# First S5 layer: inputs turned up ahead of the outputs, one token tile's GLU products moved, a fourth of Q on GpSimd

## The chip, the cores and the metric

The kernel runs on one core of one Trainium2 chip. The metric is the time of one execution on the device in microseconds (us); less is better. An engine named PE in the profile is TensorE, DVE is VectorE, ACT is ScalarE, POOL is GpSimd, and SP is the queue of SyncE, which issues most DMA transfers.

## What is computed

A trunk of four layers over 512 tokens with 1024 channels in float32: a layer with an S5 mixer, one with gated linear attention, one with differential attention and a second S5 layer, each followed by a SwiGLU FFN of hidden width 2816. The change touches only the first S5 mixer:

```python
def s5_mixer(h, lam_re, lam_im, log_dt, b_re, b_im, c_re, c_im, d_skip, w_glu):
    ...
    def chunk_step(carry, u_c):
        s_re0, s_im0 = carry
        bu_re = jnp.einsum('bcgh,gph->bcgp', u_c, bb_re)
        bu_im = jnp.einsum('bcgh,gph->bcgp', u_c, bb_im)
        ...
        _, _, s_re, s_im = lax.associative_scan(_cdiag_combine, (a_re, a_im, bu_re, bu_im), axis=1)
        s_re = s_re + p_re * s_re0[:, None] - p_im * s_im0[:, None]
        s_im = s_im + p_re * s_im0[:, None] + p_im * s_re0[:, None]
        y = jnp.einsum('bcgp,ghp->bcgh', s_re, cr) - jnp.einsum('bcgp,ghp->bcgh', s_im, ci)
        return (s_re[:, -1], s_im[:, -1]), y
    ...
    y = y + d_skip.astype(f32) * h.astype(f32)
    z = jax.nn.gelu(y).astype(h.dtype)
    a, b = jnp.split(z @ w_glu, 2, axis=-1)
    return a * jax.nn.sigmoid(b)
```

The 1024 channels are 64 groups of 16, each with a diagonal complex state of 64.

## The kernel before

The kernel is one long program, layer after layer. In the first S5 layer (`s5_first`) nothing can be prepared ahead, so the operators of the recurrence are computed beside the layer's own work. Four tokens at a time are handled as one wide step of the recurrence, so that the scan has 128 columns for each of 4 blocks.

The layer runs through eight parts of 128 channels. `s5_pipe` goes through ten steps (`kk`, called step 0 to 9 here) and in each works on several parts at once. The functions inside it, with the name by which the profile's rows can be recognised:

- `up(kk)`: four transposes turn part kk of the normed input into a PSUM bank (tile `up`, line 1392), and ScalarE copies it into `room` (line 1405).
- `products(kk)`: 16 recorded products with the input operators `inm` give V (line 1413), the inputs of the states.
- `states(kk)`, `scan`, `turn`: VectorE's rotation of V by the phases `cs` into `mods` (lines 1418 to 1423), two scans (line 1427) and four products into `prods` (lines 1436 and 1440).
- `outputs(kk)`: TensorE's y (lines 1447 and 1449) from `room` and `prods`, and ScalarE's gelu into z (line 1451; the profile calls the tile `z` or `gain`).
- `turned(kk)`: four transposes of z into a bank (tile `zp`, line 1464) and ScalarE's cast to its high half (line 1465). `rest(kk)`: VectorE's low half (line 1469). Both read the bank.
- `glu(kk)`: the products of the turned outputs with the GLU weights, for four token tiles (`NT` is 4), three products each (`mm3`, lines 420 to 422).

`s5_first` gives it hooks, functions that `s5_pipe` calls at named places of a step. They prepare the operators: `ins` turns X (tile `xps`, line 1214) and copies it into `inm` (line 1237); `phases` makes the angles (`rough`, `angle` on TensorE, lines 1032 to 1042; copies and sines on ScalarE, lines 1034 to 1050, with a table load where sines follow a gelu); `s5_rows` makes rows of the skip operator (tile `rps`, line 1180), which `s5_map` sends through DRAM; `decays` makes `r4`; `new_x` makes X on GpSimd, `new_q` makes Q. `s5_qt` turns the raw C matrices (tile `cps`, line 1118), ScalarE copies them into Q (line 1139, `base`, `Q[h][1]`), and two groups of three operations multiply them by powers (lines 1072 to 1074; `Q[h][2]` and `Q[h][3]`). There are four X and four Q, numbered h, for two parts each. `out_pads` brings Q into the output operators `oms` with four DMAs of SP's queue. `high` and `low` split the staged weights in two halves on ScalarE (line 392) and VectorE (line 400).

What sets the order: `self.hand_all()` puts all engines into an order written out by hand. Each engine does its instructions in the order in which the program emits them, and waits at each for its data and for a free buffer. PSUM has eight banks in three rings:

```python
    def acc(self, name="acc"):
        return self.ps.tile([P, 512], F32, tag="acc", name=name, bufs=4)
    def sbank(self, name="sb"):
        return self.ps.tile([P, 512], F32, tag="s", name=name, bufs=2)
    def tp(self, name="tp"):
        return self.ps.tile([P, 4, P], F32, tag="tp", name=name, bufs=2)
```

`up`, `xps`, `cps`, `rps`, y and `zp` all come from `tp`, so from two banks in turn: whoever takes one waits until the one two places before has been read. V comes from `sbank`; angles and the GLU's sums come from `acc`. The engine that multiplies Q is an argument:

```python
    def s5_q(self, eng, pool, L, b0, nb, bufs=1):
        Q = pool.tile([P, 2, nb, 5, 16], F32, tag="Q", name="Q", bufs=bufs)
        f = lambda *r: self.cross(eng, pool, L, b0, nb, *r, "dq")
```

Behind the ten steps follow the rest of the GLU (`s5_glu`) and the first FFN. The order of emission in step kk is: high(weights) in even steps, the hook "first" (rps, decays), states(kk), low(weights), outputs(kk-1), the hook "operators" (angles, xps of part kk+1), up(kk+2), turned(kk-1), products(kk+1), scans and turns, the hook "beside" (cps, Q), rest(kk-1), staging of weights, glu(kk-2).

Of the kernel before, what the change touches and what calls it, by code (L numbers as in the profile page):

```python
# [24 lines left out]
NT = SEQ // P  # L25
# [42 lines left out]
class Left:  # L68
# [4 lines left out]
    early = False  # L73
# [79 lines left out]
class Sides(Left):  # L153
# [4 lines left out]
    early = True  # L158
# [154 lines left out]
class Trunk:  # L313
# [1053 lines left out]
    def s5_pipe(self, L, hu, zT, natural, room, get, before=None, hooks=None, steps=None, left=None):  # L1367
# [4 lines left out]
        nc = self.nc  # L1372
# [14 lines left out]
        def up_first(kk):  # L1387
            ps = self.acc("up")[:].rearrange("p (b m) -> p b m", b=4) if left and kk in (1, 2, 3) else self.tp("up")[:]
            ups[kk] = ps
            for b in range(4):  # L1390
                g0 = 8 * kk + 2 * b
                nc.tensor.transpose(
                    ps[:, b], hu[:, g0 : g0 + 2].rearrange("p g t c -> p (g t c)"), self.ident[:]
                )

        def up(kk):
            if kk not in ups:
                up_first(kk)
            ps, o = ups[kk], room[kk % 4]
            if left and kk < 4:  # L1400
                v.tensor_tensor(
                    o.rearrange("p (b m) -> p b m", b=4), ps, left.Rt.unsqueeze(1).broadcast_to([P, 4, P]), op=ALU.mult
                )
            else:
                nc.scalar.copy(o, ps.rearrange("p b m -> p (b m)"))

        def products(kk):

            U, inm = room[kk % 4], get(kk, "in")
            V[kk] = [self.sbank("V"), self.sbank("V")]  # L1410
            for z in range(2):
                for b in range(4):
                    mm(V[kk][z][:, bs(b)], inm[:, z, bs(b)], U[:, bs(b)], start=True, stop=True)  # L1413

        def states(kk):

            cs, m = get(kk, "cs"), hold[kk % 2][0]
            v.tensor_tensor(m[:, 0], V[kk][0][:], cs[:, 0], op=ALU.mult)
            v.tensor_tensor(m[:, 3], V[kk][0][:], cs[:, 1], op=ALU.mult)
            v.tensor_tensor(m[:, 1], V[kk][1][:], cs[:, 1], op=ALU.mult)  # L1420
            v.tensor_tensor(m[:, 2], V[kk][1][:], cs[:, 0], op=ALU.mult)
            v.tensor_tensor(m[:, 0], m[:, 0], m[:, 1], op=ALU.add)
            v.tensor_tensor(m[:, 2], m[:, 2], m[:, 3], op=ALU.subtract)

        def scan(kk, z):
            m = hold[kk % 2][0]
            v.tensor_tensor_scan(m[:, 1 + 2 * z], get(kk, "r4"), m[:, 2 * z], 0.0, op0=ALU.mult, op1=ALU.add)
# [14 lines left out]
        def outputs(kk):  # L1442

            U, om, mop, q = room[kk % 4], get(kk, "out"), get(kk, "map"), hold[kk % 2][1]
            yb = self.tp("y")
            for b in range(4):
                mm(yb[:, b], U[:, bs(b)], mop[:, bs(b)], start=True, stop=False)
                for j in range(4):
                    mm(yb[:, b], q[:, j, b], om[:, j // 2, bs(b)], start=False, stop=j == 3)  # L1449
            z = room[4 + kk % 2].rearrange("p (t n) -> p t n", t=4)  # L1450
            nc.scalar.activation(
                z.rearrange("p t (g h) -> p g t h", h=16),
                yb[:].rearrange("p b (g t h) -> p (b g) t h", t=4, h=16), AF.Gelu_apprx_tanh,
            )
# [5 lines left out]
        def turned(kk):  # L1460
            z = room[4 + kk % 2].rearrange("p (t n) -> p t n", t=4)
            zps[kk] = zp = self.tp("zp")
            for t in range(4):
                nc.tensor.transpose(zp[:, t], z[:, t], self.ident[:])
            self.last_turned = nc.scalar.copy(dst(kk)[0], zp[:])

        def rest(kk):
            d = dst(kk)
            v.tensor_tensor(d[1], zps[kk][:], d[0].bitcast(F32), op=ALU.subtract)

        def glu(kk):
            if not accs:
                accs.extend(self.acc() for _ in range(NT))
            hl = hls[kk // 2]
            for t in range(NT):
                ts = slice(t * P, (t + 1) * P)
                self.mm3(
                    accs[t][:], zT[:, 0, kk, ts], zT[:, 1, kk, ts], hl[:, 0, kk % 2], hl[:, 1, kk % 2],
                    kk == 0, kk == KT - 1,
                )  # L1480

        if hooks:
            hook = lambda name, kk: hooks[name](kk) if name in hooks else None
            early = hooks.get("early", ())
            self.hand_all()
            if left:
                for kk in range(4):
                    up_first(kk)
            before(up, products)
            for kk in range(10):  # L1490
                if kk % 2 == 0 and kk:
                    hls[kk // 2 - 1] = self.high(stage[kk // 2 - 1], 2, 512)
                hook("first", kk)
                if kk < 8:
                    states(kk)
                if kk == 7:
                    rest(5)
                hook("ahead of low", kk)
                if kk % 2 == 0 and kk:
                    self.low(hls[kk // 2 - 1], stage[kk // 2 - 1])  # L1500
                hook("behind states", kk)
                if 1 <= kk < 9:
                    outputs(kk - 1)
                hook("operators", kk)
                late = left and kk + 2 < 4
                if kk + 2 < 8 and not late:
                    up(kk + 2)
                hook("ahead of zp", kk)
                if 1 <= kk < 9:
                    turned(kk - 1)  # L1510
                hook("behind zp", kk)
                if kk == 8:
                    glu(6)
                if kk + 1 < 8:
                    products(kk + 1)
                hook("behind products", kk)
                if kk < 8:
                    scan(kk, 0)
                    scan(kk, 1)
                    hook("behind scans", kk)  # L1520
                    for k in range(4):
                        turn(kk, k)
                if late:
                    up(kk + 2)
                hook("ahead of rest", kk)
                if kk in early:
                    rest(kk - 1)
                hook("beside", kk)
                if 1 <= kk < 9 and kk != 6 and kk not in early:
                    rest(kk - 1)  # L1530
                if kk % 2 == 0 and kk < 8:
                    stage[kk // 2] = self.staged(self.wb_src(wg, kk, D), 2, 512)
                if kk >= 2 and kk != 8:
                    glu(kk - 2)
                hook("last", kk)
            self.hand()
            return accs
# [33 lines left out]
    def s5_first(self, ctx):  # L1571
        nc, i = self.nc, self.i
# [4 lines left out]
        with self.tc.tile_pool(name="s5_0", bufs=1) as p:  # L1577
# [16 lines left out]
            X, Q, ph, r4 = {}, {}, {}, {}  # L1594
# [4 lines left out]
                    f()  # L1599

            def new_q(h):
                Q[h] = self.s5_q(nc.vector, p, 0, 8 * h, 8, 2)
                Q[h][1](self.s5_qt(raw[h][1]))

            rounded, *rows = self.s5_rows_of_phases(p)
            for y in inm:
# [33 lines left out]
            def phases(*pieces):  # L1640
                for kk, name in pieces:
                    if name == "rough":
                        ph[kk] = self.s5_phases_first(kk, cs(kk))
                    ph[kk][name]()
# [8 lines left out]
            def out_pads(kk):  # L1653
                self.s5_out_pads(oms[kk % 2], Q[kk // 2][0], slice(4 * (kk % 2), 4 * (kk % 2) + 4))
# [75 lines left out]
            def beside(kk):  # L1730
                h = kk // 2
                if kk == 2:
                    phases((7, "clip"))
                if kk % 2 == 0 and kk < 6:
                    self.s5_b_pads(bp, X[h + 1][0])
                if kk % 2 == 0 and kk < 6:
                    new_q(h + 1)
                if kk == 2:
                    phases((4, "sines"), (5, "sines"))
                if kk % 2 and kk < 7:  # L1740
                    Q[h + 1][2]()
                    Q[h + 1][3]()
                    out_pads(kk + 1)
                if kk == 1:
                    phases((4, "clip"), (5, "clip"))

            rv = {}
            hooks = {
                "first": first, "early": (2, 4), "ahead of low": ahead_of_low, "ahead of rest": ahead_of_rest, "operators": operators, "behind states": behind_states, "ahead of zp": ahead_of_zp, "behind zp": behind_zp,
                "behind products": behind_products, "behind scans": behind_scans, "beside": beside,  # L1750
            }
            accs = self.s5_pipe(0, hu, zT, True, room, get, before, hooks)
# [722 lines left out]
```

## Time and profile before

| | us |
|---|---|
| median of three runs | 2287.49 (2284.28 to 2288.44) |
| profiled execution, its own time | 2292.27 |
| its span | 2290.6 |
| TensorE busy | 2215.2 (97%) |
| VectorE busy | 1582.7 (69%) |
| ScalarE busy | 1111.4 (49%) |
| GpSimd busy | 322.7 (14%) |
| stage from 57 to 114 us: TensorE, VectorE, ScalarE, GpSimd busy | 53.63, 51.25, 37.17, 23.79 of 57 |

How to read it: a row of a timeline has the start from the span's begin, the time from the first to the last end of the merged instructions, engine, line, operation, output tile and input tiles with their shapes, and how many instructions were merged. In brackets stands how long the engine had been idle before, and what ended the wait. TensorE's products are pipelined, so that a row's length has its last product's way through the array in it; the distance from start to start tells what a group costs. In rows of a stretch of time the columns are its length, the busy time of TensorE with its instructions, the granted clock as a share of the full one, the busy share of the DMA engines and what they moved in GB/s. A matmul in float32 counts as two instructions.

### The profile page before, as it was taken

The page shows a single profiled execution, that of the slowest core. Times are in us where ns is not written, and L with a number is a line of the kernel's source. Part 1 is how long each engine was busy: PE and PEld are TensorE (multiplying, and loading weights), DVE is VectorE, ACT ScalarE, POOL GpSimd, SP SyncE. Part 2 cuts the span into 40 slices and gives each one's busy share as a digit, 9 for nine tenths or more (in the row PEclk, how much of TensorE's full clock was granted, in tenths as well). Part 3 has the DMA queues.
Part 4 walks back from the last instruction along what each step waited for, and adds up shares of the span by engine and source line. Part 5 has one row for each costly group of instructions (what it writes and reads, how often), then busy time and mean ns, then how long its engine had stood idle before and what let it go on. Part 6 is the DMA issues. An engine that isn't in the chain of part 4 may idle for free. (4 is left out here: it accounts for less than half of the span.)

```text
span 2290.6 us, 37251 instructions
## 1 busy us (share of the span) xinstructions
PE 2215.2 (97%) x14871; PEld 1966.9 (86%) x14871; DVE 1582.7 (69%) x2412; ACT 1111.4 (49%) x1779; POOL 322.7 (14%) x444
## 2 busy tenths in 40 slices
PE   6999999999999999999999999999999899999998
PEld 5888979889787799998988887899999788989997
DVE  9865878776525488777745675976766864957675
ACT  6634645444443355555435675654534223634443
POOL 5401142421000110100002231110000100101000
PEclk8999999999999999999999999999999999999999
DMA  4256666663322556765246464976641555766622
GB/s 89 59 168 170 161 158 177 162 179 89 115 76 67 147 152 175 184 172 150 94 143 147 101 148 129 234 201 146 166 101 47 143 152 147 194 174 154 169 74 74
DMA packets 294503, 319.91 MB, mean 140 GB/s; under 512 B 70141, under 2 KB 233241, under 8 KB 294202
## 3 DMA queue, kind: packets, MB, share of 16 engines
q1 hardware_dynamic: 231706, 235.79, 33.9%
q0 software_dynamic: 62624, 81.75, 19.2%
q8 instruction: 117, 1.92, 0.3%
q14 instruction: 56, 0.46, 0.1%
HBM read 285.62 MB, written 16.65 MB: 132 GB/s over the span
## 5 line engine op out<-in xcount | busy, mean ns | idle before, releaser
L400 DVE TENSOR_TENSOR whl<-wst,whl 128x1024 fp32r<-128x1024 f32 x272 | 331.9, 1225 | 273.2 <-ACT whl L392 271.1
L392 ACT CAST whl<-wst 128x1024 fp32r<-128x1024 f32 x272 | 284.5, 1051 | 345.3 <-PE acc L422 248.7
L563 PE MATMUL a<-side,whl 128*128 128x256 f32 x3168 | 382.9, 277 | 6.1 <-DVE whl L400 6.0
L563 PEld LDWEIGHTS a<-side,whl 128*128 128x128 f32 x3168 | 370.3, 188 | 7.9 <-DVE whl L400 6.8
L420 PE MATMUL acc<-whl,act 128*128 128x512 f32 x704 | 278.1, 395 | 1.7 <-DVE g L608 1.2
L421 PE MATMUL acc<-whl,act 128*128 128x512 f32 x704 | 274.9, 390 | 0.0
L422 PE MATMUL acc<-whl,act 128*128 128x512 f32 x704 | 274.8, 390 | 0.0
L563 PE MATMUL c<-side,whl 128*128 128x256 f32 x2112 | 256.2, 278 | 7.2 <-DVE whl L400 7.2
L563 PEld LDWEIGHTS c<-side,whl 128*128 128x128 f32 x2112 | 248.4, 189 | 8.2 <-DVE whl L400 8.2
L400 DVE TENSOR_TENSOR whl<-slot,whl 128x1024 fp32r<-128x1024 f32 x105 | 127.9, 1223 | 65.9 <-ACT whl L392 65.4
L420 PEld LDWEIGHTS acc<-whl,act 128*128 128x128 f32 x704 | 132.1, 188 | 31.4 <-DVE g L608 1.7
L422 PEld LDWEIGHTS acc<-whl,act 128*128 128x128 f32 x704 | 132.2, 188 | 27.9
L421 PEld LDWEIGHTS acc<-whl,act 128*128 128x128 f32 x704 | 132.2, 188 | 26.0 <-issue 0.2
L392 ACT CAST whl<-slot 128x1024 fp32r<-128x1024 f32 x105 | 110.1, 1053 | 74.4 <-PE acc L422 28.2
L420 PE MATMUL acc<-whl,hT 128*128 128x512 f32 x352 | 143.0, 406 | 1.0 <-DVE ro L2204 1.0
L422 PE MATMUL acc<-whl,hT 128*128 128x512 f32 x352 | 138.3, 393 | 0.0
L421 PE MATMUL acc<-whl,hT 128*128 128x512 f32 x352 | 138.3, 393 | 0.0
L563 PE MATMUL d<-sides,whl 128*128 128x256 f32 x1056 | 133.4, 283 | 1.3 <-ACT whl L392 1.3
L563 PE MATMUL a<-sides,whl 128*128 128x256 f32 x1056 | 134.0, 283 | 0.6 <-DVE x L546 0.6
L563 PEld LDWEIGHTS a<-sides,whl 128*128 128x128 f32 x1056 | 129.4, 191 | 1.7 <-issue 1.0
L563 PEld LDWEIGHTS d<-sides,whl 128*128 128x128 f32 x1056 | 128.9, 191 | 1.9 <-ACT whl L392 1.9
L599 POOL DMA_DIRECT2D wst<-in_ffn_w_gate_up_dram x44 | 57.1, 1297 | 441.8 <-DMA wst<-in_ffn_w_gate_up_dram 139.0
(458 smaller groups left out, 3933.4 us busy)
## 6 DMA issues: line engine op xcount, KB each, us to landing
wst<-in_ffn_w_gate_up_dram SPq DMA_DIRECT2D x88, 512.0 KB, 4.5
wst<-in_ffn_w_down_dram SPq DMA_DIRECT2D x88, 512.0 KB, 4.7
slot<-in_ffn_w_gate_up_dram SPq DMA_DIRECT2D x69, 512.0 KB, 6.2
wst<-in_ffn_w_gate_up_dram POOLq DMA_DIRECT2D x44, 512.0 KB, 6.0
halves<-in_ffn_w_gate_up_dram SPq DMA_DIRECT2D x42, 512.0 KB, 5.4
wst<-in_s_w_glu_dram SPq DMA_DIRECT2D x32, 512.0 KB, 4.8
wst<-in_gla_w_in_dram SPq DMA_DIRECT2D x24, 512.0 KB, 3.6
wst<-in_diff_w_qkv_dram SPq DMA_DIRECT2D x24, 512.0 KB, 4.3
```

Source lines behind the costliest of these rows:

```text
L392: self.last["high"] = self.nc.scalar.copy(hl[:, 0], w[:])
L400: self.last["low"] = self.nc.vector.tensor_tensor(hl[:, 1], w[:], hl[:, 0].bitcast(F32), op=ALU.subtract)
L420: mm(out, lh, rh, start=first, stop=False)
L421: mm(out, lh, rl, start=False, stop=False)
L422: self.last["mm"] = mm(out, ll, rh, start=False, stop=last)
L563: mm(o, hl[:, x, k, c], side[:, y, k], start=first and not (j or k or n), stop=k == 3 and n == 2, skip_group_check=True,)
L599: nc.gpsimd.dma_start(w[:], left.quarter(*plus, b), accum_op=ALU.add)
```

## The change

Three things are done in the first S5 layer alone; a new hook entry `apart` turns on the first two.

1. In steps 1 to 5 `up(kk+2)` is emitted at the start of the step (behind `high`, ahead of the hook "first"), no longer behind the hook "operators".
2. In steps 2 to 6 the GLU products of the first token tile, three of the twelve, are emitted behind `turned` and ahead of `products(kk+1)`; the other nine stay at the end of the step.
3. Q number 3, the last fourth, is made on GpSimd, and its two groups are emitted at once in step 4 behind its copies; before they were emitted in step 5 on VectorE. Its `out_pads` stay in step 5.

```diff
--- before.py
+++ after.py
@@ -1468,11 +1468,11 @@
             d = dst(kk)
             v.tensor_tensor(d[1], zps[kk][:], d[0].bitcast(F32), op=ALU.subtract)
 
-        def glu(kk):
+        def glu(kk, tiles=range(NT)):
             if not accs:
                 accs.extend(self.acc() for _ in range(NT))
             hl = hls[kk // 2]
-            for t in range(NT):
+            for t in tiles:
                 ts = slice(t * P, (t + 1) * P)
                 self.mm3(
                     accs[t][:], zT[:, 0, kk, ts], zT[:, 1, kk, ts], hl[:, 0, kk % 2], hl[:, 1, kk % 2],
@@ -1482,6 +1482,7 @@
         if hooks:
             hook = lambda name, kk: hooks[name](kk) if name in hooks else None
             early = hooks.get("early", ())
+            apart = hooks.get("apart", False)
             self.hand_all()
             if left:
                 for kk in range(4):
@@ -1490,6 +1491,10 @@
             for kk in range(10):
                 if kk % 2 == 0 and kk:
                     hls[kk // 2 - 1] = self.high(stage[kk // 2 - 1], 2, 512)
+                late = left and kk + 2 < 4
+                soon = apart and kk and kk + 2 < 8
+                if soon:
+                    up(kk + 2)
                 hook("first", kk)
                 if kk < 8:
                     states(kk)
@@ -1502,8 +1507,7 @@
                 if 1 <= kk < 9:
                     outputs(kk - 1)
                 hook("operators", kk)
-                late = left and kk + 2 < 4
-                if kk + 2 < 8 and not late:
+                if kk + 2 < 8 and not late and not soon:
                     up(kk + 2)
                 hook("ahead of zp", kk)
                 if 1 <= kk < 9:
@@ -1511,6 +1515,10 @@
                 hook("behind zp", kk)
                 if kk == 8:
                     glu(6)
+
+                parted = apart and 2 <= kk < 7
+                if parted:
+                    glu(kk - 2, (0,))
                 if kk + 1 < 8:
                     products(kk + 1)
                 hook("behind products", kk)
@@ -1531,7 +1539,7 @@
                 if kk % 2 == 0 and kk < 8:
                     stage[kk // 2] = self.staged(self.wb_src(wg, kk, D), 2, 512)
                 if kk >= 2 and kk != 8:
-                    glu(kk - 2)
+                    glu(kk - 2, range(1 if parted else 0, NT))
                 hook("last", kk)
             self.hand()
             return accs
@@ -1599,8 +1607,11 @@
                     f()
 
             def new_q(h):
-                Q[h] = self.s5_q(nc.vector, p, 0, 8 * h, 8, 2)
+                Q[h] = self.s5_q(nc.gpsimd if h == 3 else nc.vector, p, 0, 8 * h, 8, 2)
                 Q[h][1](self.s5_qt(raw[h][1]))
+                if h == 3:
+                    Q[h][2]()
+                    Q[h][3]()
 
             rounded, *rows = self.s5_rows_of_phases(p)
             for y in inm:
@@ -1738,15 +1749,16 @@
                 if kk == 2:
                     phases((4, "sines"), (5, "sines"))
                 if kk % 2 and kk < 7:
-                    Q[h + 1][2]()
-                    Q[h + 1][3]()
+                    if h < 2:
+                        Q[h + 1][2]()
+                        Q[h + 1][3]()
                     out_pads(kk + 1)
                 if kk == 1:
                     phases((4, "clip"), (5, "clip"))
 
             rv = {}
             hooks = {
-                "first": first, "early": (2, 4), "ahead of low": ahead_of_low, "ahead of rest": ahead_of_rest, "operators": operators, "behind states": behind_states, "ahead of zp": ahead_of_zp, "behind zp": behind_zp,
+                "first": first, "early": (2, 4), "apart": True, "ahead of low": ahead_of_low, "ahead of rest": ahead_of_rest, "operators": operators, "behind states": behind_states, "ahead of zp": ahead_of_zp, "behind zp": behind_zp,
                 "behind products": behind_products, "behind scans": behind_scans, "beside": beside,
             }
             accs = self.s5_pipe(0, hu, zT, True, room, get, before, hooks)
```

## The prediction

> **What bounds the kernel now.** I read the page first, then the waits of TensorE in the stage that is edited (44 to 150 us), then that stage's timelines engine by engine. Times are us from the start of the span, durations the second column; in brackets stands the idle time before.
>
> ```profile
> span 2290.6 us, 37251 instructions
> PE zp L1464 <- ACT inm L1237: 3.2, 5, 0.7
> PE V L1413 <- ACT inm L1237: 0.7, 1, 0.7
> ```
>
> TensorE hardly idles in this stage: once a step the turning of the outputs (zp, line 1464) waits 0.7 us for ScalarE's copies of the input operators (inm), and once, in step 6, V does (columns: total, times, longest). Those six waits, 3.9 us, are all that the change can take out on TensorE. The order around one of them, steps 1 and 2:
>
> ```profile
> 47.62 1.98 PE L1118 MATMUL cps<-ident,craw 128*64 128x128 f32 x16
> 49.52 0.80 PE L1447 MATMUL y<-scr,room 128*128 128x128 f32 x2
> ...
> 55.32 0.49 PE L1040 MATMUL angle<-counts,frow 12*128 12x512 f32 x1
> ...
> 57.68 1.15 PE L1214 MATMUL xps<-ident,X 64*64 64x64 f32 x32
> 58.76 0.66 PE L1392 MATMUL up<-ident,scr 128*128 128x128 f32 x4
> 60.10 0.66 PE L1464 MATMUL zp<-ident,gain 128*128 128x128 f32 x4 [0.68 <-ACT inm L1237]
> 60.59 1.95 PE L1413 MATMUL V<-room,inm 128*128 128x128 f32 x16
> 62.48 0.50 PE L1032 MATMUL rough<-counts,frow 12*128 12x512 f32 x1
> ...
> 63.61 0.69 PE L1180 MATMUL rps<-Q,bpad 128*32 128x64 f32 x32
> 64.23 0.49 PE L1447 MATMUL y<-scr,room 128*128 128x128 f32 x2
> ...
> 68.90 0.50 PE L1040 MATMUL angle<-counts,frow 12*128 12x512 f32 x1
> ...
> 74.16 1.95 PE L1413 MATMUL V<-room,inm 128*128 128x128 f32 x16
> ...
> 77.06 0.50 PE L420 MATMUL acc<-whl,zT 128*128 128x512 f32 x1
> ...
> 79.95 0.39 PE L1447 MATMUL y<-scr,room 128*128 128x128 f32 x2
> ...
> 106.16 0.39 PE L1447 MATMUL y<-scr,room 128*128 128x128 f32 x2
> ...
> 118.27 0.69 PE L1180 MATMUL rps<-Q,bpad 128*32 128x64 f32 x32
> ```
>
> ```profile
> 51.34 1.12 ACT L1139 ACTIVATE Q<-cps 64x128 f32<-64x128 f32 x4
> 58.88 1.17 ACT L1237 COPY inm<-xps 64x512 f32<-64x512 f32 x2 [2.06 <-PE xps L1214]
> 60.07 0.58 ACT L1405 COPY room<-up 128x512 f32<-128x512 f32 x1
> 60.80 1.10 ACT L1465 CAST zT<-zp 128x512 fp32r<-128x512 f32 x1
> 63.25 0.69 ACT L1034 ACTIVATE turns<-rough,magic 128x512 f32<-128x512 f32 x1 [1.35 <-PE rough L1033]
> ...
> 65.93 1.03 ACT L392 CAST whl<-wst 128x1024 fp32r<-128x1024 f32 x1
> 66.86 0.61 ACT L1058 COPY r<-s5r 128x512 f32<-128x512 f32 x1
> ...
> 77.18 1.13 ACT L1139 ACTIVATE Q<-cps 64x128 f32<-64x128 f32 x4 [1.73 <-PE cps L1118]
> ...
> 85.14 0.60 ACT L1451 ACTIVATE gain<-y 128x512 f32<-128x512 f32 x1
> ...
> 106.37 1.11 ACT L1139 ACTIVATE Q<-cps 64x128 f32<-64x128 f32 x4
> ```
>
> The reader is to see how these go through the two banks of the pool `tp`, handed out in turn. In order of emission they are up(2), cps(1), y(0), xps(2), up(3), zp(0), rps(1), y(1): zp(0) has the bank of xps(2), and starts at 60.10, right after the inm copies end (58.88 + 1.17 = 60.05). So the banks are the hidden resource, and each is freed by the engine that reads it, mostly ScalarE in its own order.
>
> VectorE is the second bound:
>
> ```profile
> 75.48 1.10 DVE L1469 TENSOR_TENSOR zT<-zp,zT 128x512 fp32r<-128x512 f32 x1 [2.05 <-ACT zT L1465]
> ...
> 112.02 0.69 DVE L1072 TENSOR_TENSOR Q<-Q,pw 128x512 f32<-128x512 f32 x1
> ...
> 115.28 0.69 DVE L1074 TENSOR_TENSOR Q<-Q,dq 128x512 f32<-128x512 f32 x1
> ...
> 127.16 0.69 DVE L1418 TENSOR_TENSOR mods<-V,cs 128x512 f32<-128x512 f32 x1 [0.58 <-PE V L1413]
> ```
>
> Up to 75.48 it waits for ScalarE's cast of the turned outputs; from there it has no gap until the wait ahead of 127.16. What is late at 75.48 stays late until something is taken out of VectorE.
>
> **The input turned first (steps 1 to 5).** Its four transposes (0.66) and its ScalarE copy (0.58) are only moved, with no DMA. But the order of the banks changes: now up(2), cps(1), up(3), y(0), xps(2), zp(0), up(4), rps(1), y(1). zp no longer shares with xps, so its 0.7 us wait goes. In return y gets the bank of the cps or up just ahead of it.
>
> Step 1: y(0) takes the bank of cps(1), which ScalarE empties by 51.34 + 1.12 = 52.46. It starts at 52.52 in place of 49.52, 3.0 us later. At the speed of step 2 it takes 68.90 - 64.23 = 4.67, the angles 57.68 - 55.32 = 2.36, xps to the end of the inm copies 58.88 - 57.68 + 1.17 = 2.37, and 0.05 of handing on: V at 61.97 in place of 60.59, **+1.4**.
>
> Step 2: y(1) now has the bank of up(4), whose copy stands on ScalarE behind four copies of the phases and behind the weight cast of line 392, all emitted earlier. TensorE's rough would start at 61.97 + 1.89 = 63.86; ScalarE's copies 0.77 later, at 64.63; the weight cast 65.93 - 63.25 = 2.68 after that, at 67.31; the copy of up(4) 66.86 - 65.93 = 0.93 after that, at 68.24, done at 68.82. y(1) starts at 68.88 in place of 64.23, **+4.65**. TensorE has by then done roughs (63.61 - 62.48 = 1.13), up (0.66) and rps (64.23 - 63.61 = 0.62), until 66.3, so it stands still for 2.6 us. From y(1) to V it is 4.67 + 2.36 + 2.37 + 0.05, as in step 1: V at 78.33 in place of 74.16, +4.17.
>
> **The token tile's GLU behind zp (steps 2 to 6).** Three of twelve products, a quarter of 79.95 - 77.06 = 2.89, so 0.72, go ahead of V, into the time in which TensorE would wait for inm. That cover is there (zp over at about 77.5, V at 78.33). For splitting the group I allow 0.1, an estimate: its first product is recorded with 0.50, where the twelve start 0.24 apart. In step 4 the weights' low half must be ready earlier; I get 101.9 for it and 103.4 for its user. Step 2 ends at +4.17 - 0.62 = **+3.5** (0.72 less behind V, 0.1 more).
>
> In steps 3 to 6, by the same bookkeeping: step 3 **+0.2**: ScalarE goes without a pause from the Q copies (77.18) through sines and tables to the gelu (85.14), all 4.2 later, with the copy of up(5) before it, so zp waits for the gelu about 1 us, more than the wait that it lost. Step 4 **-0.2** (0.7 less, but rps waits 0.4 for VectorE's remainder of zp, which has its bank). Step 5 **+0.7**: y(4) takes the bank of cps(3), and ScalarE empties that behind sines and tables; before, Q's copies (106.37 + 1.11) even ended after y(4)'s start (106.16). That is a wait of 1.4 in place of 0.7. Step 6 **-0.7**, the wait ahead of V. The queues' sum is **+3.5**.
>
> **Q's last fourth on GpSimd.** It takes six operations off VectorE, 112.02 to 115.28 + 0.69: 4.0 us, and issues them on GpSimd a step earlier. Nothing waits for VectorE there by then, as its next work needs zp(4)'s cast at about 119.5: gain 0. Price on GpSimd, by its nearest rows with three fourths of the elements:
>
> ```profile
> L1073 POOL TENSOR_TENSOR dx<-X,pw 128x384 f32<-128x384 f32 x4 | 3.8, 952 | 0.0
> 95.02 2.16 POOL L1074 TENSOR_TENSOR X<-X,dx 128x384 f32<-128x384 f32 x1
> ```
>
> 0.952 x 512/384 = 1.27 each, 7.6 in all; by the slowest row 2.88 each, 17.3. I take 7.6, since the group's mean covers operations beside a busy VectorE. From Q's copies at about 111.5 it is done at 119, ahead of rps(3) at 122.3. Queued behind it on GpSimd are only the decays' memset and step 6's map transfers; on SP the pads of step 6 and what follows them wait for GpSimd in place of VectorE, and their user y(6) comes at 134. Price 0, with 6.8 as the high end.
>
> **The clock.** TensorE is at half speed before y(0), and other stretches of the trace show what sends it there:
>
> ```profile
> 48.30:51.70 3.40, 3.40 (x24) 0.50 0.31 109
> 52.00:52.40 0.40, 0.40 (x6) 1.00 0.00 0
> 1396.80:1400.20 3.40, 1.73 (x8) 1.00 0.91 281
> 1400.20:1403.60 3.40, 3.40 (x13) 0.50 0.00 0
> 1789.40:1792.60 3.20, 1.40 (x13) 1.00 0.79 211
> ```
>
> It returns to full between 51.7 and 52.0, after 3.4 us full of cps and y. Now a wait of some 2 us falls into that stretch. If it returns one piece of 3.4 later (55.2), y(0) runs 2.7 us at half speed and loses 1.3; two pieces 3.0; none 0. I take **+1.3**, since the new stretch is no longer full. For the 2.6 us wait in step 2 the rows disagree: 1.7 us of idle in a stretch was followed by 3.4 us at half speed in one place, and not in the other. Half speed for 3.4 us costs **+1.7**, which I take because 2.6 is more idle than either; ends 0 and 3.4.
>
> The Trainium skill (TensorE: Matmul & The Clock Gate, "Part 1: The HAM clock gate (the "warmup" mystery)") says that the array drops to half after an idle window of about 3.4 us and returns after one busy one. By that rule neither wait is long enough to bring it down, and the sum would be near +3.5; the stretch at 1400.20 came down after less.
>
> **Sum.** 3.5 + 1.3 + 1.7 = +6.5 on the profiled execution's span, 2290.6 to 2297.1. What follows this stage keeps TensorE busy, so the delay is carried to the end. That execution took 2292.27 by its own time, 4.8 over the median of the runs, so I add to the median: 2287.5 + 6.5 = **2294.0**. 0.2%, 4.6 us, is what a measurement can tell here.
>
> **Rivals.** *The clock doesn't mind*: +3.5, 2291.0. For it: the stretch at 1789.40. Against it: the one at 1400.20.
>
> *The gap is won*: the six waits go (-3.9), the splits cost 0.5: -3.4, 2284.1; with part of VectorE's 4.0 us as well, -5.5. It needs y's bank free when TensorE comes to it in step 2, so the copy of up(4) done by 66.3 and not 68.8. For it: zp's wait was for the bank alone. Against it: the weight cast stands ahead of that copy.
>
> *GpSimd is late*: rps(3) waits if Q takes over 10.8 us from 111.5, 1.8 an operation. At 2.88 it ends at 128.8: 6.5 more on the queues' 3.5, 2297.5. One row speaks for it, the mean against it.
>
> *Nothing happens*: the waits are gone and come back elsewhere at equal size, 2287.5; step 3 is such a case.
>
> **Numbers.** The forecast 0.50, the clock unharmed 0.19, the gap won 0.15, GpSimd late 0.10, nothing 0.06. Slower: 0.50 + 0.10 = 0.60. Faster: 0.06 of the gap's 0.15, for its far end. Same: the other 0.09, 0.19 and 0.06, 0.34. The range: low 2285.0, which leaves out most of the won gap; high 2299.5, which takes in 3.5 + 3.0 + 3.4 and a little of a late GpSimd. The likeliest case alone: 2291 to 2298.
>
> **What would show it.** y of line 1447 starting at about 52.5 and then, 16 us later, behind a wait of over 2 us that ends with ScalarE's copy of up; zp without its wait for inm; half clock past 52 and again near 69; VectorE idle over 3 us ahead of the line 1469 of step 5. It is wrong if y(1) starts within 1 us of rps, or if the outputs of step 5 (106.16 now) or the rps of step 6 (118.27) come no later than before.

## The result, and the profile after

| | before | after |
|---|---|---|
| median of the runs beside each other, us | 2288.44 (7 runs) | 2296.93 (7 runs) |
| ratio of the runs, 95% interval | | 1.0042 (1.0031 to 1.0052) |
| profiled execution, its own time, us | 2292.27 | 2301.38 |
| its span, us | 2290.6 | 2299.7 |

The change made the kernel slower by 0.42%, 9.6 us by the ratio and 8.5 by the medians. The forecast was 6.5 us slower.

The first line of the page after:

```profile
span 2299.7 us, 37251 instructions
```

The waits of TensorE in the edited stage (44 to 160 us; columns: total, times, longest) show at once what came in place of the six waits of before. "Issue" means that the view saw no releaser; the timelines below show one.

```profile
PE y L1447 <- ACT room L1405: 3.2, 2, 2.6
PE y L1447 <- issue: 1.9, 1, 1.9
PE zp L1464 <- ACT gain L1451: 1.8, 2, 1.0
PE y L1447 <- ACT Q L1139: 1.2, 1, 1.2
PE zp L1464 <- ACT z L1451: 0.7, 1, 0.7
PE V L1413 <- ACT inm L1237: 0.7, 1, 0.7
```

zp no longer waits for inm. But y, which waited for nothing before, waits for ScalarE in steps 1, 2, 4 and 5. TensorE's timeline of the changed kernel, its main rows:

```profile
49.95 1.98 PE L1118 MATMUL cps<-ident,craw 128*64 128x128 f32 x16
51.86 1.12 PE L1392 MATMUL up<-ident,scr 128*128 128x128 f32 x4
54.90 0.77 PE L1447 MATMUL y<-scr,room 128*128 128x128 f32 x2 [1.92 <-issue]
...
65.92 0.66 PE L1464 MATMUL zp<-ident,gain 128*128 128x128 f32 x4
67.26 2.05 PE L1413 MATMUL V<-room,inm 128*128 128x128 f32 x16 [0.68 <-ACT inm L1237]
...
70.95 0.69 PE L1180 MATMUL rps<-Q,bpad 128*32 128x64 f32 x32
74.26 0.49 PE L1447 MATMUL y<-scr,room 128*128 128x128 f32 x2 [2.62 <-ACT room L1405]
...
90.95 0.39 PE L1447 MATMUL y<-scr,room 128*128 128x128 f32 x2
...
118.56 0.49 PE L1447 MATMUL y<-scr,room 128*128 128x128 f32 x2 [1.17 <-ACT Q L1139]
...
141.39 0.39 PE L1447 MATMUL y<-scr,room 128*128 128x128 f32 x2
```

And ScalarE's, the rows that end these waits:

```profile
53.68 1.12 ACT L1139 ACTIVATE Q<-cps 64x128 f32<-64x128 f32 x4
...
72.69 1.03 ACT L392 CAST whl<-wst 128x1024 fp32r<-128x1024 f32 x1
73.63 0.58 ACT L1405 COPY room<-up 128x512 f32<-128x512 f32 x1
...
117.39 1.12 ACT L1139 ACTIVATE Q<-cps 64x128 f32<-64x128 f32 x4
```

Step 1: Q's copies out of cps end at 54.80, y starts at 54.90. Step 2: the weight cast, then the copy of up(4) out of its bank, which ends at 74.21; y starts at 74.26. Step 5: Q's copies end at 118.51, y starts at 118.56. Each y follows the engine that empties its bank by 0.05 to 0.1 us.

The clock, by stretches of the changed kernel (columns: length, busy time of TensorE with its instructions, granted clock, busy share of the DMA engines, GB/s):

```profile
50.80:54.20 3.40, 2.18 (x16) 0.50 0.18 68
...
57.70:61.10 3.40, 3.40 (x18) 0.50 0.00 0
61.20:64.60 3.40, 3.40 (x19) 1.00 0.18 39
71.20:74.60 3.40, 0.78 (x34) 1.00 0.00 0
74.70:78.10 3.40, 3.40 (x19) 0.51 0.17 46
78.20:81.60 3.40, 3.40 (x25) 1.00 0.35 72
```

Half speed lasts to 61.1, where it ended between 51.7 and 52.0 before, and it comes back for 3.4 us right behind the wait of step 2.

In this execution step 0 already runs 2.3 us later than in the first profile (cps at 49.95, then 47.62), in code that the change leaves as it was: the clock fell there at another moment (at 27.0 and 40.6, then at 38.2). So I take the distance from that cps to the first y of step k as the mark, and call it mark k. To mark 7 it is 130.61 - 47.62 = 82.99 us before and 141.39 - 49.95 = 91.44 after: the stage itself lost 8.45.

### The profile page after: what moved, and what is told of

Same layout as the page of the kernel before. It is cut to its first block, busy times and chain, and to the rows that moved or that the text cites. A ratio compares the mean times of both kernels' runs of the same rounds, so it can differ in the third digit from the quotient of the medians.

```text
span 2299.7 us, 37251 instructions
## 1 busy us (share of the span) xinstructions
PE 2222.4 (97%) x14871; PEld 1973.7 (86%) x14871; DVE 1583.7 (69%) x2406; ACT 1111.7 (48%) x1779; POOL 333.8 (15%) x450
## 3 DMA queue, kind: packets, MB, share of 16 engines
q8 instruction: 117, 1.92, 0.3%
```

## The experiments

Where nothing else is said, a diff below is against the changed kernel. The marks of all profiled executions, us from the first cps of step 0 to the first y of steps 1, 2, 3 and 7, and the waits of TensorE ahead of y in steps 1 and 2:

| kernel | 1 | 2 | 3 | 7 | waits | ratio to before |
|---|---|---|---|---|---|---|
| before | 1.90 | 16.61 | 32.33 | 82.99 | none | |
| after | 4.95 | 24.31 | 41.00 | 91.44 | 1.92, 2.62 | 1.0042 (1.0031 to 1.0052) |
| after_again | 4.95 | 24.19 | 40.89 | 91.38 | 1.92, 2.62 | 1.0036 (1.0023 to 1.0049) |
| not_step1 | 1.90 | 19.86 | 36.56 | 87.00 | none, 2.62 | 1.0010 (0.9996 to 1.0023) |
| up_from_step3 | 1.02 | 14.82 | 30.97 | 81.38 | none | 1.0003 (0.9991 to 1.0016) |
| copy_on_vector | 5.33 | 20.67 | 35.73 | 86.16 | 3.65, 0.16 | 1.0014 (1.0001 to 1.0028) |
| filled_waits | 5.33 | 21.74 | 36.81 | 87.25 | 2.78, 0.87 | 1.0029 (1.0015 to 1.0043) |
| up_only | 5.34 | 24.58 | 41.95 | 93.76 | 3.66, 2.62 | 1.0039 (1.0026 to 1.0053) |
| glu_only | 1.02 | 14.82 | 30.54 | 81.06 | none | 0.9990 (0.9976 to 1.0004) |
| q_only | 1.90 | 16.48 | 32.20 | 83.14 | none | 1.0003 (0.9989 to 1.0017) |
| up_behind_y | 1.91 | 16.66 | 31.73 | 82.05 | none | 0.9994 (0.9982 to 1.0006) |
| up_behind_y_fill | 1.03 | 14.82 | 29.89 | 80.20 | none | 0.9997 (0.9987 to 1.0007) |

Mark 1 falls in two groups, 1.90 or 1.02 where y does not wait, and 4.95 or 5.33 where it does. That is the clock in step 0, which had come back to full before the cps in some executions and not in others, in kernels with the change and without it. Kernels are compared within a group: before, after, after_again, not_step1, q_only and up_behind_y have the half speed up to y of step 1; up_from_step3, copy_on_vector, filled_waits, up_only, glu_only and up_behind_y_fill do not. The kernel before has no profile in the second group; glu_only, whose time cannot be told from it, stands in for it there.

**up_from_step3.**

```diff
-                soon = apart and kk and kk + 2 < 8
+                soon = apart and kk > 2 and kk + 2 < 8
```

> The input is turned ahead of the outputs from step 3 on only; the split of the GLU products and Q on GpSimd stay as in the changed kernel. The mark is the distance from the first cps of step 0 to the first y of step 7: 82.99 us before the change, 91.44 after it. If the banks of y in steps 1 and 2 and the clock behind them cost the time, the two waits (1.9 and 2.6 us) and the late clock are gone: mark 83 within 0.7, time within 2 us of the kernel before. If Q on GpSimd, which slows VectorE in step 5, or the split costs it, the mark stays over 86 and the time over 3 us above the kernel before.

Mark 7 is 81.38 with a clock that was full before the cps of step 0, so it is lower than the 83 expected; glu_only has 81.06 in the same state. The ratio is 1.0003. Steps 1 and 2 carry the loss. The input turned first in steps 3 to 5, the split and GpSimd are in this kernel too and together cost nothing that can be measured.

**not_step1.**

```diff
-                soon = apart and kk and kk + 2 < 8
+                soon = apart and kk > 1 and kk + 2 < 8
```

> The changed kernel with the input turned ahead of the outputs from step 2 on, so without step 1. If both waits cost, the one of step 1 is gone and the one of step 2 stays at about 2.6 us with 1.7 us of clock behind it: y of step 2 to y of step 3 about 16.7 us as in the changed kernel (15.1 where TensorE had no such wait), and the time 3 to 5 us over the kernel before. If step 1 alone costs the time, it is within 1 us of the kernel before.

TensorE's row of y in step 2 and the clock around it, in this kernel:

```profile
67.56 0.49 PE L1447 MATMUL y<-scr,room 128*128 128x128 f32 x2 [2.62 <-ACT room L1405]
```

```profile
65.40:68.80 3.40, 1.24 (x11) 1.00 0.01 2
68.90:72.20 3.30, 3.30 (x19) 0.52 0.32 72
```

Against before, y of step 2 is 19.86 - 16.61 = 3.25 late, and mark 7 is 4.0 late. Against after_again it is 4.33 early at mark 2 and 4.4 at mark 7, so the two steps share the loss about evenly. The time's interval, 0.9996 to 1.0023, takes in no difference, but also the 4 us (1.0017) that the mark shows.

**copy_on_vector.**

```diff
+            elif hooks and hooks.get("apart") and kk == 4:
+                v.tensor_copy(o, ps.rearrange("p b m -> p (b m)"))
             else:
                 nc.scalar.copy(o, ps.rearrange("p b m -> p (b m)"))
```

> The changed kernel, with the copy of up(4) in step 2 on VectorE in place of ScalarE. If y of step 2 waits because that copy stands behind four phase copies and the weight cast on ScalarE, its wait falls from 2.6 us to under 0.5, and the clock does not fall there: mark 91.4 - 2.4 - 1.7 = 87.3 where the clock of step 1 is as in the changed kernel's profile. VectorE then starts its states some 2 us later, into a pause of 4.7 us. If something else holds y (the rows, the remainder of zp), the wait stays over 1.5 us and the mark over 89.5.

Its rows of y in steps 1 and 2 (the lines are two further down in this file), and the stretches around them:

```profile
51.65 0.77 PE L1449 MATMUL y<-scr,room 128*128 128x128 f32 x2 [3.65 <-issue]
...
66.99 0.49 PE L1449 MATMUL y<-scr,room 128*128 128x128 f32 x2 [0.16 <-DVE room L1405]
```

```profile
47.60:51.00 3.40, 0.40 (x4) 1.00 0.51 154
51.10:54.40 3.30, 2.75 (x13) 0.51 0.01 2
...
65.90:69.30 3.40, 3.24 (x55) 1.00 0.00 0
```

The wait of step 2 falls from 2.62 to 0.16 when the same copy is made by another engine. So it was ScalarE's order, neither the rows nor the remainder of zp; and the clock does not fall there. In step 1 TensorE came with a full clock, waited 3.65 us for ScalarE, and the clock fell at 51.1: a stretch with 0.40 us of work was followed by one at half speed. Mark 7 is 86.16, under the 87.3 that were expected for the other state of the clock in step 1.

**filled_waits.**

```diff
                 if soon:
+                    up_first(kk + 2)
+                    for _ in range({1: 2, 2: 4}.get(kk, 0)):
+                        for b in range(4):
+                            g0 = 8 * (kk + 2) + 2 * b
+                            nc.tensor.transpose(
+                                ups[kk + 2][:, b], hu[:, g0 : g0 + 2].rearrange("p g t c -> p (g t c)"), self.ident[:]
+                            )
                     up(kk + 2)
```

> The changed kernel, with the transposes of the turned input repeated into the same bank, twice more in step 1 and four times more in step 2, so that TensorE works through the waits ahead of y; they wait for nothing new and the data are the same. If the clock falls and stays low because of these waits, it returns in step 1 one or two pieces of 3.4 us earlier and does not fall in step 2: mark 86.7 to 88 (the queues' 3.7 alone over the 82.99 of before, and up to 1.3 of clock), time 3.4 to 4.7 us below the changed kernel. If the clock has nothing to do with the waits: mark 91.4 or more, time no better than the changed kernel.

y of step 2 in this kernel, and stretches around the waits of steps 1 and 2:

```profile
66.83 0.49 PE L1447 MATMUL y<-scr,room 128*128 128x128 f32 x2 [0.87 <-ACT room L1405]
```

```profile
45.70:49.10 3.40, 1.94 (x22) 1.00 0.62 119
49.20:52.50 3.30, 2.08 (x18) 1.00 0.13 48
...
66.30:69.60 3.30, 2.77 (x24) 1.00 0.13 37
```

y is held by the same copy, but TensorE stands still for 0.87 us and not 2.62, and the clock stays full: from mark 2 to mark 3 it is 15.07 us, where after_again has 16.70. The 1.6 us between them are the price of the clock in step 2. In step 1 this run does not tell whether the wait holds back a clock that is at half speed: its clock was full from 42.4 us on, before the added work began, so that y waited 2.78 us in spite of it. That wait is spread over two stretches, with 1.94 and 2.08 us of work, and the clock did not fall behind it. Mark 7, 87.25, is in the range expected if the waits make the clock fall (86.7 to 88), yet not for the reason given for step 1: with a full clock TensorE comes sooner and waits longer for ScalarE. The time is some 3 us under the changed kernel's (1.0029 against 1.0042, with overlapping intervals), a little less than the 3.4 to 4.7 expected.

**after_again** (the changed kernel as it is).

> The changed kernel once more, for the clock. If the waits ahead of y make the clock fall, half speed appears again after y of step 1 has waited (from about 51 to 62 us) or behind the wait of step 2, and the time is 7 to 10 us over the kernel before. If the half speed of the first profile was chance, this profile shows none past the start of y in step 1, and y of step 1 then waits longer for ScalarE, over 2.5 us, because TensorE comes to it sooner.

It shows the half speed from 38.1 to 58.5 and for 3.4 us from 72.2, and the marks of the first profile to 0.12 us. Two of its stretches, at the end of the long half speed:

```profile
55.10:58.50 3.40, 3.40 (x18) 0.50 0.01 2
...
58.60:62.00 3.40, 3.40 (x19) 1.00 0.16 33
```

Step 0 has the timing of the kernel before here (cps at 47.73, there 47.62; half speed there from 38.2), so the pair shows the change alone: 91.38 - 82.99 = 8.4 us.

**up_only** (`parted = False`, Q as before).

> Only the first part of the change: the input turned first in steps 1 to 5, with the GLU products undivided behind V and Q on VectorE. If the divided products fill the hole ahead of V, that hole is now open: V waits for inm by 0.6 to 0.7 us in steps 1 to 6, and from y of step 3 to y of step 7 it is 50.4 + 4 x 0.6 = 52.8 us. If they fill nothing, 50.4 us. The time is then 10 to 12 us over the kernel before, or 7 to 10.

The wait that the split fills, in this kernel:

```profile
PE V L1413 <- ACT inm L1237: 3.8, 6, 0.7
```

V waits for inm in six steps, as expected, but from mark 3 to mark 7 it is 51.81, between the two forecasts (50.49 in after_again, 52.8 expected). The split is worth 1.3 us, half of what was reckoned, since with V later the waits of zp in step 3 and of y in step 5 for ScalarE shrink, from 1.03 to 0.35 and from 1.18 to 0.49. (Q is on VectorE here as well; q_only below shows that this neither costs nor gains.) The time, 1.0039 or 8.9 us over the kernel before, is under the 10 to 12 us expected if the split fills the hole. In step 1 y waits 3.66 us at a full clock, and half speed follows from 49.3 to 56.2.

**glu_only** (`soon = False`, Q as before).

> Only the divided GLU products, with the input turned where it was and Q on VectorE. zp keeps its wait for inm in steps 1 to 5 (0.7 us), since it shares the bank with xps, and only step 6 gains 0.7: mark from y of step 3 to y of step 7 50.66 - 0.7 + 4 x 0.1 = 50.4 us, time within 1 us of the kernel before. If dividing costs more than 0.1 a step, it is over 51 us.

```profile
PE zp L1464 <- ACT inm L1237: 2.9, 5, 0.7
```

zp keeps its waits; from mark 3 to mark 7 it is 50.52, near the 50.4 expected, and the time cannot be told from before.

**q_only** (the third part alone, put into the kernel before).

> The kernel before with only Q's last fourth on GpSimd. If its cost is hidden, as the forecast has it, the mark is 83 to 83.5 and the time within 1.5 us of the kernel before; VectorE loses six operations in step 5 but its scan and products there run up to twice as long beside GpSimd, as in the changed kernel, so that it gains nothing either. If the late Q is a cost, rps of step 6 waits for GpSimd by over 1 us and the mark is over 84; if VectorE was a bound, the mark falls under 82.

Q on GpSimd, the first and the last of its six operations in this kernel:

```profile
107.19 2.41 POOL L1072 TENSOR_TENSOR Q<-Q,pw 128x512 f32<-128x512 f32 x1 [5.09 <-ACT Q L1139]
...
116.22 1.64 POOL L1074 TENSOR_TENSOR Q<-Q,dq 128x512 f32<-128x512 f32 x1
```

It takes from 107.19 to 117.86, 10.7 us, and mark 7 is 83.14: no gain and no cost, and rps of step 6 (at 118.44) does not wait for it.

**up_behind_y.** If the cause is the banks, the intent of the change can be had in another order: the input turned behind y, ahead of xps (the edit that leaves Q on VectorE is not printed).

```diff
-                soon = apart and kk and kk + 2 < 8
-                if soon:
-                    up(kk + 2)
+                soon = apart and kk > 1 and kk + 2 < 8
...
                     outputs(kk - 1)
+                if soon:
+                    up(kk + 2)
                 hook("operators", kk)
```

> A version that keeps what the change is after: in steps 2 to 5 the input is turned behind the outputs but ahead of xps, so that y has the bank that it had before, and zp shares with the turned input and not with xps; the GLU products are divided as in the change, Q stays on VectorE. If the banks are the whole story, y waits for ScalarE in no step, neither zp nor V waits for inm in steps 2 to 6, and from y of step 2 to y of step 7 it is 66.4 us as before less 0.7 in step 6 and 0.2 to 0.5 in steps 2 to 5, so 64 to 65; VectorE, without a gap from step 3 on, may hold it at 65.5. The time is 1 to 2.5 us under the kernel before, which may be too little to tell.

Its waits in the stage:

```profile
PE xps L1214 <- ACT gain L1451: 1.9, 2, 1.6
...
PE zp L1464 <- ACT inm L1237: 0.7, 1, 0.7
```

y waits nowhere, zp for inm only in step 1, and V not at all. From mark 2 to mark 7 it is 65.39 against 66.38: 1.0 us won, less than the 1.4 to 2.4 expected, as xps now waits 1.6 us in step 3 for the gelu, which ScalarE reaches behind the sines and two table loads. The ratio, 0.9994 with its interval, does not tell it from the kernel before. Its clock fell at 27.0 and at 40.6 as in the first profile of the changed kernel; here half speed ended at 54.3, there at 61.1.

A second version of it repeated the transposes of the second and third input in pauses ahead of step 0:

```diff
             ps, o = ups[kk], room[kk % 4]
+            if hooks and hooks.get("apart") and kk in (1, 2):
+                for b in range(4):
+                    g0 = 8 * kk + 2 * b
+                    nc.tensor.transpose(
+                        ps[:, b], hu[:, g0 : g0 + 2].rearrange("p g t c -> p (g t c)"), self.ident[:]
+                    )
```

> The same, with the transposes of the second and third turned input done twice, in pauses of TensorE of 0.9 and 0.5 us ahead of step 0. If the half speed between 38 and 52 us of the kernel before comes from such pauses, it is gone or shorter in more of the runs, and the time another 1 to 3 us lower. If it comes from the small products of the phases, which leave most of the array idle, nothing changes.

Its time is no better than up_behind_y's, and half speed showed for twice 6.8 us, from 26.7 and from 40.3. The pauses that I filled were not the cause, or not alone; what sends the clock down ahead of step 0 stays open.

## Why the prediction was right

The direction, the mechanism and the places were as forecast; one term was too small.

- **Step 1, the bank of cps**: y was to start 3.0 us late; against the first cps it starts 4.95 - 1.90 = 3.05 late.
- **Step 2, the copy of up(4) on ScalarE**: a standstill of 2.6 us was forecast, 2.62 measured, ended by the named copy. Without step 1, y was to be 4.65 - 1.4 = 3.25 late; not_step1 has 3.25. In copy_on_vector, where another engine makes the same copy, the wait is 0.16.
- **Steps 3 to 6** were to cancel (0.2 - 0.2 + 0.7 - 0.7): from mark 3 to mark 7 it is 50.66 before and 50.44 after. Step by step, from V to V as the forecast counts, after_again is 0.28 later than before in step 3, 0.19 earlier in step 4, 0.77 later in step 5 and 0.56 earlier in step 6. The waits are 1.03 ahead of zp in step 3 and 1.17 ahead of y in step 5, as named, and 0.56 ahead of y in step 4. That last one is for the copy of up(6), where I had named rps and VectorE: the size of step 4 came out by luck.
- **The clock in step 2**: +1.7 forecast, 1.6 by filled_waits. All four profiles with the wait of 2.62 us, of three kernels, show half speed behind it; the two in which the wait was taken away or filled do not.
- **The clock in step 1** is the term that was mis-sized. I let it return one piece of 3.4 us later (+1.3) and kept two pieces as the high end (+3.0). Half speed ended at 51.8 in the kernel before and at 58.5 in after_again, which began in the same state: 6.7 us later, two pieces. What step 1 adds at mark 2, 4.33 by after_again and not_step1, is its 1.4 of queues and these 3.0. With 3.0 for it the sum is 3.5 + 3.0 + 1.7 = 8.2, and the stage lost 8.4. My reason, that the stretch was no longer full, holds for the next one as well: in the first profile y waits from 53.0 to 54.9, which takes from the stretch 50.80:54.20 and from the one behind it, and the clock is back after the first full one. That fits both profiles, but it is argued: no run shortened that wait at half speed, and the kernel before was at half speed through full stretches too.
- **The split** was to fill V's hole and cost 0.1 a step; in steps 2 to 6 V waits for inm in up_only and not in the changed kernel. The split was worth 1.3 us, about half of the 2.4 reckoned for up_only; glu_only's 50.52 fits the 0.1 a step.
- **Q on GpSimd** was forecast at 7.6 us with no gain and no cost. It took 10.8, hidden all the same; that it cost nothing was in part luck. The margin was thin, as the changed kernel's rows of GpSimd, VectorE and TensorE show:

```profile
118.01 2.57 POOL L1072 TENSOR_TENSOR Q<-Q,pw 128x512 f32<-128x512 f32 x1 [6.11 <-DVE mods L1422]
...
127.18 1.64 POOL L1074 TENSOR_TENSOR Q<-Q,dq 128x512 f32<-128x512 f32 x1
```

```profile
118.52 3.14 DVE L1427 TENSOR_TENSOR_SCAN mods<-r,mods 128x512 f32<-128x512 f32 x2
121.58 1.47 DVE L1440 TENSOR_TENSOR prods<-mods,cs 128x508 f32<-128x508 f32 x1
122.97 1.75 DVE L1436 SCALAR_TENSOR_TENSOR prods<-mods,cs 128x508 f32<-128x508 f32 x1
124.65 3.00 DVE L1440 TENSOR_TENSOR prods<-mods,cs 128x508 f32<-128x508 f32 x2
127.57 1.08 DVE L1469 TENSOR_TENSOR zT<-zp,zT 128x512 fp32r<-128x512 f32 x1
```

```profile
129.71 0.69 PE L1180 MATMUL rps<-Q,bpad 128*32 128x64 f32 x32
```

Q ends at 128.82, 0.9 us ahead of rps, so the rival of a late GpSimd did not come about. The same scans and products of VectorE in step 5 of the kernel before:

```profile
107.40 2.34 DVE L1427 TENSOR_TENSOR_SCAN mods<-r,mods 128x512 f32<-128x512 f32 x2
109.65 0.67 DVE L1440 TENSOR_TENSOR prods<-mods,cs 128x508 f32<-128x508 f32 x1
110.23 0.68 DVE L1436 SCALAR_TENSOR_TENSOR prods<-mods,cs 128x508 f32<-128x508 f32 x1
110.82 1.28 DVE L1440 TENSOR_TENSOR prods<-mods,cs 128x508 f32<-128x508 f32 x2
```

I forecast a VectorE idle over 3 us ahead of line 1469 of step 5; there is no such pause, because its scans and products in that step took 9.05 us beside GpSimd (118.52 to 127.57), where before they took 4.62 (107.40 to 112.02). VectorE lost 4.0 us of work and got 4.4 us of slowness back, a term that the prediction did not have.

The rival in which the gap is won fell: its condition, that the copy of up(4) is done before TensorE has finished rps, fails by 2.6 us. The rival in which the clock does not mind (+3.5) fell too: 1.6 us in step 2 and about 3 in step 1 are clock. "Nothing happens" fell with the interval of the result, 1.0031 to 1.0052.

Two slips of the prediction change nothing: the high end of GpSimd's price stands there once as 6.8 and once as 6.5 (17.3 - 10.8 is 6.5), and the stretch at 1789.40 has 1.8 us of idle, not 1.7.

## What to carry to other kernels

Moving an operation earlier in a hand-made order also moves its turn in a ring of buffers, and the operations around its old and its new place get other neighbours. Before such a move, write down the ring in both orders and ask, for each pair that shares a buffer, which engine empties it and what that engine has queued ahead. A wait of 2 us on TensorE may also cost the clock behind it: here 1.6 us behind a wait of 2.62, and about 3 where a wait of 1.92 fell into half speed.

## What the runs showed of the hardware

- The clock of TensorE falls for 3.4 us, or whole multiples, behind some stretches in which it had little work but was not idle throughout: 0.40 us of 3.40 in copy_on_vector, 0.78 in the changed kernel, 0.89 in up_only and 1.24 in not_step1 were followed by half speed. The amount of work in a stretch does not settle it: 1.73 us of 3.40 in the kernel before was followed by half speed, and 1.40 of 3.20 there and 1.94 and 2.08 in filled_waits were not. The Trainium skill (TensorE: Matmul & The Clock Gate, Part 1) gives the same pieces of 3.4 us, but speaks of an idle window. Here part of one was enough.
- The Trainium skill (TensorE: Matmul & The Clock Gate, Part 1) also says that one busy window brings the clock back. The kernel before stays at half speed from 38.2 to 51.8 while TensorE counts as busy in every stretch; why is open.
- When the clock of TensorE falls ahead of step 0 differs from execution to execution of one kernel: at 27.0 and 40.6 in the first profile of the changed kernel, at 38.1 in after_again, and the first cps starts at 49.95 and 47.73. Over all profiles it starts between 45.0 and 50.0. Comparing distances from an operation close to the edit took most of this out; what was left are the two groups of mark 1.
- VectorE is slower beside GpSimd's products of 128x512: in q_only its two scans take 3.14 us and its first product 1.47, in the same step of the kernel before 2.34 and 0.67. Six such products took 10.7 and 10.8 us on GpSimd; whether they would be faster alone no run shows.
